# Feed-forward first product on scaled fp16 halves, with weight sums formed by adding transfers

## Chip, cores and metric

The kernel runs as one program on one core of a Trainium2 chip. The metric is the device time of one launch in microseconds (us). Three runs of the kernel before gave 2275.92 to 2276.97 us, median 2276.76.

## What is computed

Two layers of an encoder on 1024 positions of width 1024, fp32 in and out. Each layer is attention with a convolution module beside it, then a gated feed-forward block:

```
y = concatenate([y_attn, u]) @ w_o[l];  x = x + y
h2 = rmsnorm(x, g_ffn[l])
z = dwconv(h2 @ w_up[l], w_dw_ffn[l], b_dw_ffn[l])     # w_up: 1024 x 5632
zg, zv = split(z, 2)
x = x + (silu(zg) * zv) @ w_down[l]                    # w_down: 2816 x 1024
```

The change concerns `h2 @ w_up[l]`, the feed-forward block's first product.

## The kernel before

**Exact products from parts.** A fp32 operand is split into a high part, rounded to the reduced fp32 type F32R, and a low part, the rest. A product is three matmuls: high by high, high by low, low by high.

**Seven products for eight.** For block f (of 22: 128 gate columns and 128 value columns) the weights lie as four quarters, gate or value (e = 0, 1) by half of the contraction (h = 0, 1). A scheme of Strassen's kind makes two halves of the positions of both gate and value from seven products instead of eight, in the order `ORDER = (1, 5, 6, 3, 7, 2, 4)`. Products 1, 2 and 4 take a quarter as it is; 5, 6, 3 and 7 take sums and differences of quarters (weights) and of quarters of h2 (the "mixed sets" 5, 3, 6, 7, 4). Products 6, 7, 4 and 3 add onto a PSUM bank that already holds an earlier product of the block, so that the eviction in between (`evict`, L1124) must come first. One product is 12 matmuls of 128x128 by 128x512 (`product`, L1112 to L1122; the matmul is L1120) and fills one *step*.

**Order.** `feed` (L899) has a list of steps, TensorE's work, and a table of work put behind a step with a rank, written out by hand: `put(step, rank, f)`. Every engine's queue runs in program order. Steps 0 to 15 are the w_o stage (`wo_steps`, L933), where h2 is normed (`norm`, L996; `first`, L1001, for sets 1 and 2 in steps 12 to 15) and the mixed sets are made (`combine`, L1006, at the steps of `MIX_AT`, 18 to 31). Then 154 steps are the up-projection (`up_steps`, L1061): first those of `START` (L90: products 1 and 2 of blocks 0 to 3, then the others of blocks 0 to 3 as their sets come), then block after block. Below, n is the step of a block's product 1. The down-projection follows (`down_steps`, L1238), in the same scheme with its own combinations (`combine`, L1283) and evictions (`evict_end` L1316, `evict` L1327).

**Weights of blocks 4 to 21.** SP's queue fetches both rows of quarters (512 KB each, `fetch`, L1071) at n - 8. VectorE forms the sums in place (L1078, through `sub`, L1069). Products 5 and 6 take their parts from `pair` (L1494): ScalarE rounds, VectorE subtracts (L1499). Products 3 and 7 (`part`, L1082) and 1, 2 and 4 (`cast` and `turn`, L1093) get the low part by a transfer: a GpSimd DMA writes the high part, rounding on the way (`cast_pair`, L891, DMA at L894), or ScalarE does; then `complete` (L188) has ScalarE write the high part's negative (L189) and a GpSimd DMA add the source to it from HBM (L190).

**Beside it.** In eleven blocks of each layer (7 to 12 and 14 to 18) a pair of rows of the down weights is loaded (`sum_load`, L1170), summed in four steps on VectorE (`sum_step`, L1175) and stored for the later stage. The convolution over z, silu and the product of gate and value run on ScalarE and VectorE (L1146 to L1168). In the mixing stage, `value_squares` and `value_scale` (L858, L866) make a power-of-two scale for the attention's value weights from the sum of their squares; TensorE sums over partitions by a matmul with ones (L870).

Of the kernel before, what the change touches and what calls it, by code (L numbers as in the profile page):

```python
# [9 lines left out]
F32 = mybir.dt.float32  # L10
# [40 lines left out]
P_GKV = 11  # L51
# [20 lines left out]
P_SCALE = 32768.0  # L72
TURNED_BY_DMA = ()
# [23 lines left out]
TAIL_STEPS = 6  # L97
ENDS = (slice(512, 768), slice(768, T))
# [27 lines left out]
class Encoder:  # L126
# [257 lines left out]
    def run(self):  # L384
# [4 lines left out]
        self.ones = self.cp.tile([128, 128], F32, name="ones")  # L389
        nc.vector.memset(self.ones, 1.0)  # L390
        self.ones_r = self.cp.tile([128, 128], F32R, name="ones_r")
# [9 lines left out]
    def first_sections(self, l, supply):  # L401
# [58 lines left out]
        nc.vector.tensor_copy(out=self.ones_r, in_=self.ones)  # L460
# [87 lines left out]
    def project(self, l, carry):  # L548
# [264 lines left out]
        scales = {1: lambda: st.update(squares=self.value_squares(l, w["v"])),  # L813
                  2: lambda: st.update(scale=self.value_scale(l, st.pop("squares")))}
# [43 lines left out]
    def value_squares(self, l, w):  # L858
        f = self.cp.tile([128, 8], F32, name=f"vf{l}", tag="vf", bufs=1)
        for k in range(2):  # L860
            t = self.blk(f"vsq{l}_{k}")[:, 0:512]
            self.nc.scalar.activation(out=t, in_=w[0][:, k * 512:(k + 1) * 512].bitcast(F32), func=AF.Square,
                                      scale=self.par[l][:, P_GKV + k:P_GKV + k + 1], accum_out=f[:, k:k + 1])
        return f

    def value_scale(self, l, f):  # L866
        nc = self.nc
        ps = self.bank(f"vf{l}p", (128, 1))
        for k in range(2):
            nc.tensor.matmul(ps, self.ones, f[:, k:k + 1], start=k == 0, stop=k == 1)  # L870
        h, s, r = (f[:, i:i + 1] for i in (2, 3, 4))
        nc.vector.tensor_scalar(out=h.bitcast(I32), in0=ps.bitcast(I32), scalar1=24, scalar2=None, op0=ALU.logical_shift_right)
        nc.vector.tensor_scalar(out=s.bitcast(I32), in0=h.bitcast(I32), scalar1=-8388608.0, scalar2=200 * 8388608.0, op0=ALU.mult, op1=ALU.add)
        nc.vector.tensor_scalar(out=r.bitcast(I32), in0=h.bitcast(I32), scalar1=8388608.0, scalar2=39 * 8388608.0, op0=ALU.mult, op1=ALU.add)
        return s, r
# [57 lines left out]
    def wo_steps(self, l, conv, ys, w, casts, x, steps, put):  # L933
        nc, a, par = self.nc, self.a, self.par[l]
        left, right = HALVES
        casts, ps, acc, sq, rf, us = {(1, m): e for m, e in casts.items()}, {}, {}, {}, {}, []
# [59 lines left out]
        def norm(c, k):  # L996
            xk = x[k, c]
            nc.vector.scalar_tensor_tensor(out=xk, in0=xk, scalar=par[:, P_GFFN + k:P_GFFN + k + 1], in1=rf[c],
                                           op0=ALU.mult, op1=ALU.mult)

        def first(k):  # L1001
            norm(0, k)
            i = 1 + k // 4
            sets[i].append(self.pair(x[k, 0], f"b{l}_{i}{k}", "m", True))

        def combine(i, ks, srcs):  # L1006
            for o, p, q in srcs:
                if q is not None:
                    nc.vector.tensor_tensor(out=o, in0=p, in1=q, op=ALU.subtract)
            pairs = [self.tmp("b", f"b{l}_{i}{k}", F32R, (128, 2, 512)) for k in ks]  # L1010
# [31 lines left out]
        for k in range(8):  # L1042
# [6 lines left out]
        plan = ((5, 0, b11, b12, b11), (3, 4, b22, b22, None), (6, None, b11, b22, b11), (7, None, b12, b22, b12),  # L1049
                (4, None, b21, b21, b11))  # L1050

        def mix(i, j, o, p, q, ks):
            for k in ks if j is not None else ():
                norm(1, k + j)
            combine(i, ks, [(o(k), p(k), q(k) if q else None) for k in ks])
# [5 lines left out]
    def up_steps(self, l, steps, put):  # L1061
# [6 lines left out]
        raw, wts, casts, st, sums = defaultdict(dict), {}, {}, defaultdict(dict), {}  # L1068
# [6 lines left out]
        def quarters(f):  # L1075
            return [raw[f][e][:, h] for e in range(2) for h in HALVES]

        def combine(f, o, p, q, op=ALU.subtract):  # L1078
            z = quarters(f)
            sub(z[o], z[p], z[q], op)  # L1080

        def part(i, f):  # L1082
            a11, a12, a21, a22 = quarters(f)
            src = {1: a11, 2: a12, 5: a21, 6: a21, 7: a11, 3: a12}[i]
            if i == 7 or f < 2 or i == 3 and f >= LEFT:
                t = self.tmp("ws", f"w{l}_{f}_{i}", F32R, (128, 2, 512))
                nc.scalar.copy(out=t[:, 0], in_=src)
                self.complete(None, t[:, 0], t[:, 1], src)
            else:
                t = self.pair(src, f"w{l}_{f}_{i}", "ws")  # L1090
            wts[i, f] = t[:, 0], t[:, 1]

        def cast(i, f):  # L1093
            e, h = {1: (0, 0), 2: (0, 1), 4: (1, 1)}[i]
            casts[i, f] = self.cast_pair(a["w_up"][l, f + e * NF][:, HALVES[h]], f"w{l}_{f}_{i}", "b" if i == 4 and f >= LEFT else "ws")

        def turn(i, f):
            wts[i, f] = self.complete(*casts.pop((i, f)))

        def first_cast(f):  # L1100
            casts[f] = self.cast_tile(a["w_up"][l, f], f"wc{l}_{f}", "b" if f == 1 else "ws")

        def first_turn(f):
            hi, lo = self.complete(*casts.pop(f))
            for i, c in enumerate(HALVES):
                wts[1 + i, f] = hi[:, c], lo[:, c]
# [5 lines left out]
        def product(i, f):  # L1112
            z, w = st[f], wts.pop((i, f))
            if i in (1, 5, 2):
                z[i] = bank(i, f)
            ps = z[{6: 1, 7: 1, 4: 1, 3: 5}.get(i, i)]
            for k in range(4):
# [6 lines left out]
        def evict(i, f):  # L1124
            z = st[f]
            if i == 1:
                z["g"] = self.blk(f"zg{l}_{f}")
                nc.scalar.copy(out=z["g"][:, left], in_=z[1])
            elif i == 5:
                z["v"] = self.blk(f"zv{l}_{f}")  # L1130
                nc.scalar.copy(out=z["v"][:, right], in_=z[5])
            elif i in (6, 3):
                src = z[1] if i == 6 else z.pop(5)
                if (i == 3) == (f < LEFT):
                    nc.scalar.copy(out=z["g"][:, right], in_=src)
                else:
                    sub(z["g"][:, right], src, z["g"][:, right], ALU.add)
            elif i == 7:
                sub(z["v"][:, right], z[1], z["v"][:, right], ALU.add)
            elif i == 2:  # L1140
                sub(z["g"][:, left], z.pop(2), z["g"][:, left], ALU.add)
            elif i == 4:
                nc.scalar.copy(out=z["v"][:, left], in_=z.pop(1))

        def filter_start(f, e):
            z = st[f]  # L1146
# [4 lines left out]
        def filter_tap(f, e, t):  # L1151
            z = st[f]
            self.conv_tap(l, e * NF + f, z["ov"[e]], z["in", e], 0, T, t)

        def keep(f):
            st[f]["src"] = st[f].pop("v")

        def silu(f):
            o = st[f]["o"]
            nc.scalar.activation(out=o, in_=o, func=AF.Silu)  # L1160

        def close(f):
            z = st.pop(f)
# [19 lines left out]
        for f, e, n, tag in ((0, 0, 4, "wr"), (1, 0, 5, "wr"), (0, 1, 6, "wr"), (1, 1, 9, "b"),  # L1183
                             (2, 1, 22, "b"), (2, 0, 22, "b"), (3, 0, 24, "b"), (3, 1, 24, "wr")):
            put(n, 5, lambda f=f, e=e, tag=tag: fetch(f, e, tag))
        for f in range(1, LEFT):
            n = 10 + f if f == 1 else 11 + f
            put(n, 4, lambda f=f: first_cast(f))
            put(n + 2 + f // 3, 4, lambda f=f: first_turn(f))
        for i in (1, 2):  # L1190
            put(13, 0.5, lambda i=i: part(i, 0))
        for q, (i, f) in enumerate(seq):
# [4 lines left out]
            if i == 4 or i < 3 and f >= LEFT:  # L1197
                early = 2 if i == 4 and f < 2 else 0
                put(n - (9 if f >= LEFT else 7) - early, 1.5, lambda i=i, f=f: cast(i, f))
                put(n - 5 - early, 4, lambda i=i, f=f: turn(i, f))  # L1200
            elif i > 2 and f < LEFT:
                m = {5: 18, 3: 20, 6: 24, 7: 27}[i] if f < 2 else n - {5: 3, 3: 4, 6: 6, 7: 6}[i]
                put(m, 0.5 if f < 2 else 4, lambda i=i, f=f: part(i, f))
                if i == 5:
                    put(17 if f < 2 else m - 1, (0.5 if f < 2 else 3), lambda f=f: (combine(f, 0, 0, 2), combine(f, 2, 2, 3, ALU.add)))
# [736 lines left out]
```

## Time and profile before

| | |
|---|---|
| median of three runs | 2276.76 us |
| the profiled execution | 2276.63 us |
| its span, first to last instruction | 2274.9 us |
| granted TensorE clock, mean | 0.999 |
| w_o stage, layer 0 / 1 | 406 to 504 / 1533 to 1632 us |
| up-projection | 504 to 926 / 1632 to 2053 us |
| down-projection | 926 to 1137 / 2053 to 2267 us |

How to read the profile: PE is TensorE's matmuls, PEld its weight loads, DVE VectorE, ACT ScalarE, POOL GpSimd, SP the engine that only issues DMAs. "L1120" is the line of the kernel's file. A group's row reads line, engine, operation, output <- inputs, shape, count, then busy time, mean length of one in ns, and idle time ahead of it with what ended it. A matmul's own length overlaps the next one's: what counts is the distance from start to start. Of the DMA queues, q0 is GpSimd's software queue and q1 the hardware queue of SP; "to landing" is from issue to completion.

### The profile page before, as it was taken

Reading aid. Unit: us, or ns where it says so; the run is one execution under the profiler, and the core shown is the slowest. Engines: PE = TensorE matmul, PEld = TensorE weight load, DVE = VectorE, ACT = ScalarE, POOL = GpSimd, SP = SyncE. Lnnn points to the kernel's source line nnn. Section 1 sums busy time; section 2 is a strip of 40 time slices with the busy share of each in tenths; the row PEclk is TensorE's granted clock in tenths of the full one; section 3 lists DMA queues with packets and bytes.
Section 4 is the critical chain, followed back from the end, with each engine's and each line's share of the span. In section 5 each row is a group of like instructions: output and inputs, shape, how many; then the busy total and the mean of one; then the engine's idle time right before and its main releaser. Section 6 shows DMA issues by size and latency. Waiting matters only on the chain.

```text
span 2274.9 us, 30440 instructions
## 1 busy us (share of the span) xinstructions
PE 2264.2 (100%) x10690; PEld 1834.8 (81%) x10690; DVE 1738.7 (76%) x2305; ACT 1298.0 (57%) x2058; POOL 783.0 (34%) x812
## 2 busy tenths in 40 slices
PE   9999999999999999999999999999999999999999
PEld 8887777788888888888888877777888888888888
DVE  7989888868877676776559788887697777768765
ACT  5355977646655555544533578784475555555444
POOL 1222797532333333001412237963323333320032
PEclk9999999999999999999999999999999999999999
DMA  6888998856899998935968999867669999989356
GB/s 194 168 180 260 199 207 177 212 151 141 208 281 297 275 297 203 333 106 144 207 139 167 215 255 201 188 150 208 174 132 231 269 300 278 294 208 320 105 121 171
DMA packets 199144, 475.72 MB, mean 209 GB/s; under 512 B 27232, under 2 KB 35280, under 8 KB 198992
## 3 DMA queue, kind: packets, MB, share of 16 engines
q0 software_dynamic: 103136, 222.46, 48.6%
q1 hardware_dynamic: 95568, 250.80, 32.9%
q8 instruction: 84, 1.38, 0.3%
q14 instruction: 68, 0.56, 0.1%
q10 hardware_dynamic: 288, 0.53, 0.1%
HBM read 309.29 MB, written 80.40 MB: 171 GB/s over the span
## 4 chain that ended last, share of the span: by engine, by line
PE 93%; issue 2%; DVE 2%; DMA 1%; ACT 1%; SPq 0%; POOL 0%; DVEq 0%; POOLq 0%; ACTq 0%
PE p L1120 36%; PE pd L1308 18%; PE po L931 7%; PE s L1564 7%; PE t L1604 4%; PE o L1627 4%; PE pq L226 3%; PE pa L226 3%; PE pkv L226 2%; PE pg L226 2%; PE pg L545 2%; PE pa L545 1%; PE pk L226 1%; PE pn L226 1%; PE pkr L759 1%
## 5 line engine op out<-in xcount | busy, mean ns | idle before, releaser
L1120 PE MATMUL p<-b,w 128*128 128x512 f32 x3552 | 807.0, 389 | 0.6 <-DVE zv L1069 0.5
L1120 PEld LDWEIGHTS p<-b,w 128*128 128x128 f32 x3552 | 666.3, 188 | 140.6 <-DVE zv L1069 0.9
L1308 PE MATMUL pd<-ab,wd 128*128 128x512 f32 (+1 forms) x1920 | 422.2, 381 | 0.0
L1308 PEld LDWEIGHTS pd<-ab,wd 128*128 128x128 f32 x1920 | 350.8, 188 | 69.4 <-DVE ab L1499 0.4
L190 POOL DMA_DIRECT2D w<-wu x96 | 84.8, 886 | 360.5 <-ACT w L189 310.0
L1564 PE MATMUL s<-k,q 96*128 96x512 f32 x768 | 207.7, 406 | 0.8 <-ACT p L1574 0.8
L1607 DVE SCALAR_TENSOR_TENSOR pt<-t,pt 128x512 f16<-128x512 f32 x256 | 164.8, 684 | 38.9 <-ACT pt L1606 38.3
L1796 POOL TENSOR_TENSOR late<-gate,par 128x1014 f32<-128x1014 f32 (+12 forms) x79 | 171.6, 2172 | 12.4 <-PE pn L226 12.4
L1606 ACT ACTIVATE pt<-t 128x512 f16<-128x512 f32 x256 | 139.2, 596 | 57.0 <-PE t L1604 56.0
L1511 DVE SCALAR_TENSOR_TENSOR o<-zg,par,o 128x1023 f32<-128x1023 f32 x88 | 112.8, 1283 | 76.5 <-ACT o L1505 75.2
L190 POOL DMA_DIRECT2D w<-in_w_up x116 | 100.5, 867 | 199.2 <-ACT w L189 175.3
L1566 DVE TENSOR_REDUCE mx<-s 128x1 f32<-128x1024 f32 x128 | 155.7, 1217 | 1.3 <-PE s L1564 1.3
L1564 PEld LDWEIGHTS s<-k,q 96*128 96x128 f32 x768 | 135.2, 189 | 23.6 <-ACT p L1574 1.3
L1574 ACT ACTIVATE p<-s,mx 128x1024 f32<-128x1024 f32 x128 | 143.2, 1118 | 4.4 <-DVE mx L1566 4.0
L1779 DVE SCALAR_TENSOR_TENSOR conv<-gate,par,conv 128x1009 f32<-128x1009 f32 (+7 forms) x112 | 142.3, 1274 | 3.7 <-ACT conv L607 1.0
L1604 PEld LDWEIGHTS t<-ident,p 128*128 128x128 f32 x1024 | 119.8, 141 | 25.2 <-DVE yt L1634 0.8
L894 POOL DMA_DIRECT2D wd<-in_w_down x44 | 32.8, 754 | 306.6 <-PE pd L1308 306.4
L1497 ACT CAST ab<-ac 128x512 fp32r<-128x512 f32 x130 | 80.1, 617 | 97.5 <-DVE ac L1243 94.8
L189 ACT ACTIVATE w<-w 128x512 fp32r<-128x512 f32 x212 | 133.5, 630 | 3.0
L1627 PE MATMUL o<-pt,v 128*128 128x512 f16 x512 | 132.8, 381 | 1.2 <-DVE pt L1607 1.1
L1604 PE MATMUL t<-ident,p 128*128 128x128 f32 x1024 | 133.2, 273 | 0.1
L1069 DVE TENSOR_TENSOR zg<-p,zg 128x512 f32<-128x512 f32 x88 | 60.5, 690 | 95.1 <-PE p L1120 88.4
(2117 smaller groups left out, 4083.9 us busy)
## 6 DMA issues: line engine op xcount, KB each, us to landing
w<-in_w_up POOLq DMA_DIRECT2D x232, 256.0 KB, 7.3
wu<-in_w_up SPq DMA_DIRECT2D x88, 512.0 KB, 5.7
w<-wu POOLq DMA_DIRECT2D x96, 256.0 KB, 5.9
sd<-in_w_down SPq DMA_DIRECT2D x44, 512.0 KB, 9.9
ws<-sd SPq DMA_DIRECT2D x44, 512.0 KB, 7.0
wd<-in_w_down POOLq DMA_DIRECT2D x88, 256.0 KB, 5.4
act<-v SPq DMA_DIRECT2D x36, 512.0 KB, 5.8
ac<-act SPq DMA_DIRECT2D x72, 256.0 KB, 6.1
```

The source lines that it names most:

```text
L190: self.nc.gpsimd.dma_start(out=lo, in_=src, accum_op=ALU.add)
L226: nc.tensor.matmul(ps[:, HALVES[c]], w, x[:, HALVES[c]], start=(k == 0 and s == 0), stop=(k == n - 1 and s == 2))
L931: self.nc.tensor.matmul(ps, p[:, sl], q[:, cs], start=(k == 0 and t == 0), stop=(k == 3 and t == 2))
L1120: nc.tensor.matmul(ps, w[p][:, k * 128:(k + 1) * 128], b[:, q], start=(i in (1, 5, 2) and k == 0 and t == 0), stop=(k == 3 and t == 2), sk ...
L1308: nc.tensor.matmul(ps[t, m][:, cs], w[i, j][p][:, m * 128:(m + 1) * 128], b[:, q, cs], start=(i in (1, 5, 2) and j == 0 and s == 0), stop= ...
L1564: nc.tensor.matmul(ps[:, cs], q[i][0:96, qs], k[j][0:96, cs], start=(s == 0), stop=(s == 2))
L1566: nc.vector.tensor_reduce(out=mx, in_=ps, op=ALU.max, axis=AX.X, negate=True)
L1574: nc.scalar.activation(out=p, in_=ps, func=AF.Exp, bias=mx, accum_out=st["sums"][:, qt:qt + 1])
L1604: nc.tensor.transpose(tp[:, i, qi * 128:(qi + 1) * 128], st["p"][2 * qp + qi][:, kt * 128:(kt + 1) * 128], self.ident)
L1607: nc.vector.scalar_tensor_tensor(out=lo, in0=tp, scalar=P_SCALE, in1=hi, op0=ALU.mult, op1=ALU.subtract)
L1627: nc.tensor.matmul(po, v[2 * c + i][:, h // 2, e, :], pt[s][:, 2 * (c % 2) + i, :], start=(c == 0 and i == 0 and s == 0), stop=(c == 3 and ...
L1796: self.nc.gpsimd.tensor_tensor(out=p[:, lo:hi], in0=u[:, lo + s:hi + s], in1=self.tap(l, j, t).broadcast_to([128, hi - lo]), op=ALU.mult)
```

## The change

1. **fp16 parts.** The products of L1120 take fp16 high and low parts of both operands. h2 is scaled by a power of two through its gain (`scales`, from the squares of the gain, in the same small matmul as the value weights' scale). Each block's weights get a power-of-two scale from the sum of their squares: two Squares of 1,024 columns on ScalarE, a matmul with ones, five one-column operations on VectorE. ScalarE writes the scaled high part (`upper`), VectorE the low part (`lower`). The evictions multiply the scale back out. No part of w_up is cast or completed by transfer any more.
2. **Value rows' sign turned.** Some products, and the quarters of z that they make, carry the other sign, so that every sum of weight quarters is an addition. The down-projection's combinations and evictions turn it back.
3. **Sums by adding transfers.** The sums for products 5, 6, 3 and 7 are formed by GpSimd DMAs that add a quarter from HBM to the fetched one in SBUF. The down weights' sums are formed by GpSimd DMAs that add one half in SBUF to another, four per pair of rows; step offsets 0, 3, 3, 6 and 9 (the store) in place of 1, 1, 2 and 6.
4. **Mixed sets.** The low parts of all sets are subtracted on GpSimd (before: sets 1 and 2 alone).
5. **Blocks 0 to 3.** Their rows are fetched at steps 0 to 4, squared two steps later, and have one sum and one set of scales at step 7; they are fetched a second time for the sums.
6. **Times.** For blocks 4 to 21: fetch n - 14, squares n - 11 and n - 10, first sum n - 10, total n - 8, scale n - 7, parts from n - 7 to n + 3.

The core of the diff:

```diff
         def combine(i, ks, srcs, sign):
...
-                if i in MIX_ADDED:
-                    self.complete(None, t[:, 0], t[:, 1], src[0])
-                else:
-                    nc.vector.tensor_tensor(out=t[:, 1], in0=src[0], in1=t[:, 0].bitcast(F32), op=ALU.subtract)
+                nc.gpsimd.tensor_tensor(out=t[:, 1], in0=src[0], in1=t[:, 0], op=ALU.subtract)
...
+        def add_in(dst, src):
+            nc.gpsimd.dma_start(out=dst, in_=src, accum_op=ALU.add)
+
+        def sum5(f):
+            add_in(raw[f][1][:, left], block(f, 1, 1))
...
+        def squares(f, e, out):
+            t = self.blk(f"wsq{l}_{f}{e}", F16)
+            nc.scalar.activation(out=t, in_=raw[f][e], func=AF.Square, accum_out=out)
...
+        def own_total(f):
+            st["total", f] = self.pp.tile([128, 2], F32, name=f"wt{l}_{f}", tag=f"d{6 + (f > LEFT and (f + 1) % 2)}", bufs=1)
+            nc.tensor.matmul(st["total", f], self.ones, st["sums", f][:, 6:8], start=True, stop=True)
...
+        def upper(t, src, f):
+            nc.scalar.activation(out=t, in_=src, func=AF.Copy, scale=scale[f])
+
+        def lower(t, src, hi, f):
+            nc.vector.scalar_tensor_tensor(out=t, in0=src, scalar=scale[f], in1=hi, op0=ALU.mult, op1=ALU.subtract)
...
         def sum_step(j, n):
             p, q = sums[j]
-            sub(*((p[:, left], p[:, left], p[:, right]), (p[:, right], p[:, right], q[:, right], ALU.add),
-                  (q[:, right], q[:, right], p[:, left]), (q[:, left], q[:, left], q[:, right]))[n])
-            if n == 3:
-                for e, t in enumerate(sums.pop(j)):
-                    nc.sync.dma_start(out=self.wsd[l][j, e], in_=t)
+            if n < 4:
+                add_in(*((p[:, left], p[:, right]), (p[:, right], q[:, right]), (q[:, right], p[:, left]), (q[:, left], q[:, right]))[n])
+                return
+            for e, t in enumerate(sums.pop(j)):
+                nc.sync.dma_start(out=self.wsd[l][j, e], in_=t)
...
         for f in range(LEFT, NF):
-            n = at[1, f]
+            n = at[1, f] + 2 * (f == LEFT)
             for e in range(2):
...
+                at_step(n - 14, 5 + e / 10, fetch, f, e, "b" if e else "wr")
+                at_step(n - 11 + e, 2, own_squares, f, e)
+            at_step(n - 10, 2.1, sum5, f)
+            at_step(n - 8 + (f == LEFT), 0.4, own_total, f)
+            at_step(n - 7 + (f == LEFT), 0.5, own_scale, f)
+            for i, m in ((5, -6 if f == LEFT else -7), (6, -3), (4, -2), (3, 1), (7, 2)):
+                at_step(n + m, 3.6, part_hi, i, f)
+                at_step(n + m + 1, 3.5 if i != 6 else 1, part_lo, i, f)
+                if i in (5, 6):
+                    at_step(n + m + 1, 3.55, (sum6, sum3)[i - 5], f)
```

More of the change, by code (lines that the diff above doesn't have):

```diff
@@ L866, in value_scale @@
-    def value_scale(self, l, f):
-        nc = self.nc
[L868 to L875, printed above, removed]
+            nc.scalar.activation(out=t, in_=w[0][:, k * 512:(k + 1) * 512].bitcast(F32), func=AF.Square,
+                                 scale=par[:, P_GKV + k:P_GKV + k + 1], accum_out=f[:, k:k + 1])
@@ L1067, in up_steps @@
         self.kept = {}
-        raw, wts, casts, st, sums = defaultdict(dict), {}, {}, defaultdict(dict), {}
+        raw, wts, zs, st, sums, scale, back, nback = defaultdict(dict), {}, defaultdict(dict), {}, {}, {}, {}, {}
         sub = lambda o, p, q, op=ALU.subtract: nc.vector.tensor_tensor(out=o, in0=p, in1=q, op=op)
@@ L1093, in cast, with block @@
[L1093 to L1106, printed above, removed]
+        def block(f, e, h):
+            return a["w_up"][l, f + e * NF][:, HALVES[h]]
@@ new lines, in scales @@
+        def scales(ps, out, w):
+            ps = ps.rearrange("p (f e) -> p f e", e=2)
+            scale, back, nback, v, h = (out[:, i * w:(i + 1) * w] for i in range(5))
+            nc.vector.tensor_reduce(out=v, in_=ps, op=ALU.add, axis=AX.X)
+            self.half_exponent(h, v)
+            self.power(scale, h, -1.0, 204.0)
+            for o, at in ((back, self.back), (nback, self.nback)):
+                nc.vector.tensor_scalar(out=o.bitcast(I32), in0=h.bitcast(I32), scalar1=EXPONENT, scalar2=at, op0=ALU.mult, op1=ALU.add)
+            return scale, back, nback
@@ new lines, in first_total, with first_squares @@
+        def first_total():
+            ps = self.bank(f"wt{l}", (128, 2 * LEFT))
+            tags = self.banks[1][0]
+            tags.insert(0, tags.pop())
+            nc.tensor.matmul(ps, self.ones, st["sums"], start=True, stop=True)
+            parts = scales(ps, self.cp.tile([128, 5 * LEFT], F32, name=f"wt{l}", tag="wt", bufs=1), LEFT)
+            for f in range(LEFT):
+                scale[f], back[f], nback[f] = (t[:, f:f + 1] for t in parts)
+        def first_squares(f, e):
+            if "sums" not in st:
+                st["sums"] = self.cp.tile([128, 2 * LEFT], F32, name=f"wa{l}", tag="wa", bufs=1)
+            squares(f, e, st["sums"][:, 2 * f + e:2 * f + e + 1])
@@ new lines, in upper, with part_hi, part_lo, both @@
+        def upper(t, src, f):
+            nc.scalar.activation(out=t, in_=src, func=AF.Copy, scale=scale[f])
+        def lower(t, src, hi, f):
+            nc.vector.scalar_tensor_tensor(out=t, in0=src, scalar=scale[f], in1=hi, op0=ALU.mult, op1=ALU.subtract)
+        def part_hi(i, f):
+            upper(operand(i, f)[:, 0], source(i, f), f)
+        def part_lo(i, f):
+            hi, lo = wts[i, f]
+            lower(lo, source(i, f), hi, f)
+        def both(f):
+            return st[(1, 2), f], raw[f][0].rearrange("p (i c) -> p i c", i=2)
@@ L1108, in bank, with first_hi, first_lo @@
+        def first_hi(f):
+            for i in (1, 2):
+                operand(i, f)
+            t, src = both(f)
+            upper(t[:, :, 0], src, f)
+        def first_lo(f):
+            t, src = both(f)
+            lower(t[:, :, 1], src, t[:, :, 0], f)
         def bank(i, f):
```

211 lines of the change are left out of this document (126 added, 85 removed).

## The prediction

> **What bounds the kernel now.** First the engine totals and the chain of waits of the profile before.
>
> ```profile
> PE 2264.2 (100%) x10690; PEld 1834.8 (81%) x10690; DVE 1738.7 (76%) x2305; ACT 1298.0 (57%) x2058; POOL 783.0 (34%) x812
> ...
> PE 93%; issue 2%; DVE 2%; DMA 1%; ACT 1%; SPq 0%; POOL 0%; DVEq 0%; POOLq 0%; ACTq 0%
> PE p L1120 36%; PE pd L1308 18%; PE po L931 7%; PE s L1564 7%; PE t L1604 4%; PE o L1627 4%; PE pq L226 3%; PE pa L226 3%; PE pkv L226 2%; PE pg L226 2%; PE pg L545 2%; PE pa L545 1%; PE pk L226 1%; PE pn L226 1%; PE pkr L759 1%
> ```
>
> TensorE is busy all through, and its own instructions are 93% of the chain that ends last; the line that the change rewrites, L1120, is 36% of the span. Every nanosecond of TensorE's cadence counts, and other work costs something only where it makes TensorE wait. The table by stage shows, for layer 0, the four stretches that the change reaches: the w_o stage, the start of the up-projection, its steady part, and the down-projection.
>
> ```profile
> 406.00:504.00 98.00, 97.29 (x452) 78.83 (x451) 67.30 (x104) 46.36 (x74) 38.73 (x42) 1.00 0.67 184
> 504.00:583.00 79.00, 78.92 (x353) 64.86 (x352) 69.42 (x105) 52.23 (x86) 21.39 (x28) 1.00 0.69 156
> 583.00:926.00 343.00, 342.48 (x1511) 283.25 (x1510) 244.42 (x300) 191.85 (x290) 103.99 (x137) 1.00 0.97 266
> 926.00:1137.00 211.00, 211.00 (x936) 174.74 (x936) 146.04 (x231) 102.26 (x178) 35.43 (x50) 1.00 0.66 189
> ```
>
> Columns: stretch, its length, busy time of TensorE, of its weight load, of VectorE, ScalarE and GpSimd, the granted clock (1.00, so no throttle), the DMA engines' busy share, GB/s. In the start, VectorE is at 69.42 of 79 us. In the steady part it is at 244.42 of 343 and ScalarE at 191.85, but the DMA engines are at 0.97: the resource that is closest to taking over from TensorE.
>
> **TensorE's own part.** The timeline of TensorE has one row with 45 products of L1120 in a run, and one with eight fp16 matmuls of the same size in a run, each with weights of its own; the groups give the length of one:
>
> ```profile
> 695.83 10.36 PE L1120 MATMUL p<-b,w 128*128 128x512 f32 x45
> ```
>
> ```profile
> 412.50 1.89 PE L1627 MATMUL o<-pt,v 128*128 128x512 f16 x8
> ```
>
> ```profile
> L1120 PE MATMUL p<-b,w 128*128 128x512 f32 x3552 | 807.0, 389 | 0.6 <-DVE zv L1069 0.5
> ...
> L1627 PE MATMUL o<-pt,v 128*128 128x512 f16 x512 | 132.8, 381 | 1.2 <-DVE pt L1607 1.1
> ```
>
> From start to start a fp32 matmul takes (10.36 - 0.389) / 44 = 226.6 ns, a fp16 one (1.89 - 0.381) / 7 = 215.6 ns. The program has 22 blocks x 7 products x 12 matmuls x 2 layers = 3,696 of them, and as many after. Gain: 3,696 x 11.0 ns = **-40.7 us**.
>
> Added on TensorE are the sums of squares over partitions: a matmul of ones with two or eight columns, 18 + 1 per layer, 38 in all; the two calls per layer that sum the value weights' squares become one, so 36 more calls. The nearest rows are those two present calls, four passes, in TensorE's timeline:
>
> ```profile
> 191.18 0.50 PE L870 MATMUL vf0p<-vf,ones 128*128 128x1 f32 x4
> 191.54 0.72 PE L226 MATMUL pn<-cqs_0h,wu10h 128*128 128x512 f32 x2
> ```
>
> The next product starts 0.36 us after the first pass, so 0.18 us per call: 36 x 0.18 = **+6.5 us**. The sums go beside nothing; all of it counts.
>
> **VectorE, ScalarE, GpSimd.** The groups, each form apart, give the price of one operation:
>
> ```profile
> L1607 DVE SCALAR_TENSOR_TENSOR pt<-t,pt 128x512 f16<-128x512 f32 x256 | 164.8, 684 | 38.9 <-ACT pt L1606 38.3
> ...
> L1574 ACT ACTIVATE p<-s,mx 128x1024 f32<-128x1024 f32 x128 | 143.2, 1118 | 4.4 <-DVE mx L1566 4.0
> ...
> L189 ACT ACTIVATE w<-w 128x512 fp32r<-128x512 f32 x212 | 133.5, 630 | 3.0
> ...
> L1499 DVE TENSOR_TENSOR ab<-ac,ab 128x512 fp32r<-128x512 f32 x130 | 89.2, 688 | 22.7 <-ACT ab L1497 15.6
> ...
> L1574 ACT ACTIVATION_READ_ACCUMULATOR p<-s,mx 128x1 f32 x128 | 26.8, 209 | 0.0
> ...
> L1499 POOL TENSOR_TENSOR b<-y,b 128x512 fp32r<-128x512 f32 x16 | 24.2, 1625 | 28.1 <-ACT b L1497 28.1
> ...
> L745 DVE SCALAR_TENSOR_TENSOR qn<-qn,qns 128x1024 fp32r<-128x1024 f32 x8 | 15.5, 1944 | 2.4 <-ACT qns L743 2.4
> ...
> L1779 DVE SCALAR_TENSOR_TENSOR conv<-gate,par,conv 128x1020 f32<-128x1020 f32 x8 | 10.2, 1279 | 0.2
> ```
>
> VectorE loses 264 sums of weight halves, 84 lows of weights and 40 of mixed sets (0.69 us each), and gains 220 lows of 512 columns (0.684, as L1607, fp16 out as well), 44 of 1,024 (1.28, as L1779) and some 190 one-column operations (taken at 0.21, the shortest row here): -268 + 150 + 56 + 40 = -22 us. ScalarE loses 212 negations and some 186 casts (0.63), and gains 220 scaled uppers of 512 columns (0.63), 44 of 1,024 and 88 squares of 1,024 (1.12, and 0.21 to read the accumulator): -251 + 139 + 49 + 117 = +54 us. Both are spread over some 840 us of products. In the steady part neither comes near TensorE's pace: nothing, unless one of these in-order queues stands at a transfer, since the eviction that TensorE needs before it adds to a bank again is queued behind it (see the chain of transfers).
>
> GpSimd takes over 20 lows of mixed sets per layer, in the start. L745 runs while GpSimd combines tensors and has a mean of 1.94 us, where L1779, as wide and also with both inputs in SBUF, takes 1.28 us: the two engines hinder each other. The Trainium skill, "SBUF — State Buffer", section "Who interferes with whom", has the rule: a VectorE instruction with two SBUF inputs contends with a GpSimd instruction that reads SBUF, and the one that comes second waits out the whole instruction. The two means agree; no row shows it in the start, and the rule speaks against this move. The price in both layers: at best nothing (20 x 0.69 = 13.8 us per layer leave VectorE). At worst VectorE waits out each, 20 x 1.625 = 32.5 us, against 79 - 69.4 + 13.8 = 23.4 us of room: 9 us per layer, **18 us** in all. I take **+3 us**, near the lower end: sets are mixed at steps 18 to 31 of the stage, three to six steps (12 x 0.2266 = 2.72 us each) ahead of their products, so most of the waiting fits. In this are the eight squares per layer in the w_o stage, where ScalarE has 98 - 46 = 52 us of room.
>
> Turned signs in the down-projection change operators, not counts (0.69 us before and after): nothing.
>
> **DMA.** Two windows of the transfers: four blocks of the steady part, in each of which a half of the down weights is summed as well, and a cast that stands alone (4 us).
>
> ```profile
> DMA packets 8418, 22.33 MB, mean 290 GB/s; under 512 B 932, under 2 KB 932, under 8 KB 8412
> ...
> q0 software_dynamic: 4605, 8.39, 53.0%
> q1 hardware_dynamic: 3807, 13.87, 50.1%
> ...
> w<-in_w_up POOLq DMA_DIRECT2D x24, 256.0 KB, 9.5
> wu<-in_w_up SPq DMA_DIRECT2D x8, 512.0 KB, 7.2
> ws<-sd SPq DMA_DIRECT2D x8, 512.0 KB, 8.3
> sd<-in_w_down SPq DMA_DIRECT2D x8, 512.0 KB, 10.5
> w<-wu POOLq DMA_DIRECT2D x10, 256.0 KB, 7.3
> act<-v SPq DMA_DIRECT2D x4, 512.0 KB, 6.5
> ```
>
> ```profile
> q0 software_dynamic: 144, 0.26, 24.5%
> ...
> wd<-in_w_down POOLq DMA_DIRECT2D x1, 256.0 KB, 3.0
> ```
>
> The window (773 to 850 us) is 77 us long. A hardware transfer of 512 KB takes 0.501 x 77 / 28 = 1.38 us of all engines; 34 software transfers take 0.530 x 77 / 34 = 1.20 us each. A cast alone took 0.245 x 4 = 0.98 us; with 12 casts among the 34, an adding transfer takes (40.8 - 11.8) / 22 = 1.32 us. Per such block before: 5 adding, 3 casts, 7 hardware = 6.6 + 2.9 + 9.7 = 19.2 us against TensorE's 84 x 0.2266 = 19.0. After: 4 adding for the up-weights, 4 for the down-weights' sums, the same 7: 10.6 + 9.7 = **20.2 us against 84 x 0.2156 + 0.18 = 18.3**. (The shares add to 103% in that window, because packets of both queues overlap on an engine, so 1.03 is what was carried without loss.) At 1.03 a block takes 19.6 us, 1.3 more than TensorE: there are 11 of them per layer, in runs of six and five, and the seven others need only 4 adding and 3 hardware transfers (9.4 us) and make up ground. Bounds: nothing, if more than 1.03 can be carried or the lag stays in the lead (fetches are issued 14 steps ahead, each sum three steps, 7.8 us, ahead of its reader), up to 2 x (11 x 1.3 - 2 x 1.3) = **23 us**, with only 7.8 - 6.5 = 1.3 us of lead per run (6.5: next row). No row says where between, so I take the middle: **+11 us**.
>
> **The chain of transfers on GpSimd.** The adding transfers' line in the steady part:
>
> ```profile
> L190 POOL DMA_DIRECT2D w<-wu x34: 889/893/1255, 601.2 to 906.6; - x34
> ...
>   ACT w L189: 200.4, 81
> ...
> DMA to landing us min/median/max: 3.3/6.5/10.0
> ```
>
> GpSimd spends 200 us there waiting for ScalarE's negations; these waits go. New ones come: the down weights' sums are formed in place by transfers, each needing the one before: the second must have landed before the third writes what the second reads, and so on. All issue from GpSimd's one in-order queue, so a block takes at least 3 landings plus an issue of 0.9 us; queued behind are the up-weights' sums, which ScalarE waits for, then evictions, then TensorE. At 18.3 us the break-even is a landing of (18.3 - 0.9) / 3 = **5.8 us**. The median of before, 6.5, lies above; but it was reached with several transfers under way, (24 x 9.5 + 10 x 7.3) / 77 = 3.9 by the window's rows, and in the chain each starts with one or two ahead of it. Nearer to it is the middle between 3.3 and 6.5, 4.9 us: 15.6 us a block, hidden. Cost: nothing, upper bound in rival C.
>
> **Sum.** Against the profiled execution, 2276.63 us (its span is 2274.9; the median of the runs is 0.13 higher): 2276.6 - 40.7 + 6.5 + 3 + 11 = **2256 us**.
>
> **Rivals.**
> The page's DMA issues, both layers:
>
> ```profile
> w<-in_w_up POOLq DMA_DIRECT2D x232, 256.0 KB, 7.3
> ...
> w<-wu POOLq DMA_DIRECT2D x96, 256.0 KB, 5.9
> ```
>
> H, all hidden: 2276.6 - 40.7 + 6.5 = 2242 us. For it: VectorE gets lighter and the transfers of the whole stage fewer (88 + 44 adding per layer in place of (232 + 96) / 2 = 164 software transfers). Against: 20.2 us of transfers in 18.3.
> S, the start stalls: VectorE and GpSimd lock each other out at their worst, 2242 + 11 + 18 = 2271 us. For it: 69.42 of 79 and L745's mean. Against: the room of some steps.
> C, slower than before: the chain on GpSimd takes the place of TensorE as the bound. With a landing of 6.5 us a block takes 20.4 us, 2.1 over; 2 x (11 x 2.1 - 2 x 1.3) = 41 us: 2242 + 3 + 41 = 2286 us, and with 7.3 us (w<-wu in the window above) 4.5 us a block, 94 us, 2339. It decides from 5.8 us on.
> N, the change doesn't do what it says: fp16 holds 215.6 ns only over eights, and in long runs keeps 226.6. 2276.6 + 6.5 + 11 = 2294 us at most. Against: no row shows what would hold it back.
>
> **How the numbers follow.** Chances: forecast 0.34 (own range 2248 to 2267), H 0.17, S 0.12, C 0.29, N 0.05, worse than all 0.03. About 0.2%, 4.5 us, can be told from no change: from 2272.2 to 2281.3. Faster: forecast, H and 0.07 of S, 0.58. Same: 0.05 of S and 0.04 of C (landing just over the break-even), 0.09. Slower: 0.25 of C, N and the rest, 0.33. The range runs from H to a C at 6.6 us: 2241 to 2292; beyond lie 0.10 of C, half of N and the rest, and a little of H, 0.18.
>
> **What would show it.** Products at about 215.6 ns in long runs and 38 small sums near 0.18 us (else N). In the dense windows of the steady part, idle TensorE with ScalarE waiting for the transfers into the raw weights: by full DMA engines (share 0.99, GpSimd not waiting) the forecast; with GpSimd standing at the down weights' landings, C. Idle TensorE in the start before (3, 0), (6, 0) with lows late on GpSimd: S. The forecast is wrong if TensorE is idle under 3 us in all or over 30.

## The result and the profile after

The changed kernel takes 2372.73 us (median of four runs, 2370.92 to 2374.02) against 2276.86 us for the kernel before: ratio 1.042, 95% interval 1.0402 to 1.0438. It is 96 us slower, where 21 us less was forecast; the range ended at 2292.

The page of the changed kernel: engine totals, the chain that ended last, and the groups and transfers that answer to those shown of before (L1208 is the product, L1099 all adding transfers, L1169 and L1172 the high and low parts of the weights).

```profile
PE 2270.6 (96%) x10762; PEld 1517.9 (64%) x10762; DVE 1759.2 (74%) x2384; ACT 1364.9 (58%) x2104; POOL 803.8 (34%) x776
...
PE 62%; DMA 16%; issue 8%; DVE 6%; POOL 5%; ACT 4%; POOLq 0%; SPq 0%; DVEq 0%; ACTq 0%
PE pd L1405 18%; DMA sd<-sd 11%; PE p L1208 11%; PE s L1665 6%; PE po L949 4%; PE t L1705 4%; PE o L1728 3%; DMA wu<-in_w_up 3%; PE pq L228 3%; PE pa L228 3%; PE pkv L228 2%; PE pg L228 2%; DVE w L1172 2%; PE pg L546 1%; POOL sd L1099 1%
...
L1208 PE MATMUL p<-b,w 128*128 128x512 f16 x3696 | 843.6, 389 | 83.3 <-ACT zg L1215 60.3
...
L1099 POOL DMA_DIRECT2D sd<-sd x88 | 78.2, 953 | 268.9 <-DMA sd<-sd 259.2
...
wu<-in_w_up POOLq DMA_DIRECT2D x176, 256.0 KB, 7.0
...
sd<-sd POOLq DMA_DIRECT2D x88, 256.0 KB, 7.9
```

TensorE's share of the chain falls from 93% to 62%, and the line that bounded the kernel from 36% to 11%. In its place stands a transfer, `sd<-sd`, the down weights' sums: 11%, and GpSimd waits 259 us for them. The table by stage, for layer 0 again:

```profile
406.00:510.00 104.00, 102.84 (x479) 81.48 (x477) 76.31 (x115) 57.71 (x93) 41.04 (x45) 1.00 0.71 199
510.00:590.00 80.00, 70.24 (x314) 31.14 (x313) 58.62 (x77) 46.68 (x72) 34.16 (x31) 0.96 0.41 92
590.00:970.00 380.00, 347.11 (x1568) 155.87 (x1567) 258.16 (x351) 220.22 (x305) 100.79 (x114) 0.96 0.88 224
970.00:1182.00 212.00, 212.00 (x941) 175.13 (x939) 145.88 (x231) 102.98 (x179) 34.97 (x50) 1.00 0.66 184
```

The loss lies in the up-projection: TensorE idles 10 us in the start and 33 us in the steady part, and the granted clock, 1.00 before, is 0.96 in both. VectorE and ScalarE are far from full. Six blocks of the steady part (7 to 12), one row each:

```profile
656.90:675.10 18.20, 18.20 (x87) 8.39 (x88) 13.53 (x19) 12.34 (x17) 5.25 (x6) 1.00 0.89 205
675.10:693.40 18.30, 18.30 (x90) 8.49 (x89) 13.71 (x19) 12.12 (x17) 5.72 (x8) 1.00 0.95 246
693.40:718.90 25.50, 20.74 (x90) 8.97 (x89) 13.62 (x19) 12.34 (x17) 8.45 (x10) 0.87 0.99 255
718.90:738.60 19.70, 18.65 (x87) 8.31 (x88) 13.71 (x19) 12.34 (x17) 6.61 (x8) 1.00 0.97 254
738.60:761.10 22.50, 18.67 (x89) 8.31 (x88) 13.81 (x19) 12.32 (x17) 6.43 (x9) 1.00 0.97 252
761.10:784.60 23.50, 19.82 (x89) 8.75 (x88) 13.71 (x19) 12.36 (x18) 7.68 (x10) 0.93 0.99 255
```

Blocks without a hold-up take the forecast 18.3 us. Sums start at block 7; after two blocks the lead is used up and a block takes 19.7 to 25.5 us. GpSimd's timeline over a block shows what paces it (each row a group of issues, in brackets the wait ahead of it):

```profile
720.33 1.78 POOL L1099 DMA_DIRECT2D sd<-sd  x2 [2.80 <-DMA sd<-sd]
725.07 0.88 POOL L1099 DMA_DIRECT2D wu<-in_w_up  x1 [2.96 <-DVE w L1172]
731.72 0.89 POOL L1099 DMA_DIRECT2D sd<-sd  x1 [5.77 <-DMA sd<-sd]
735.53 0.88 POOL L1099 DMA_DIRECT2D sd<-sd  x1 [2.93 <-DMA sd<-sd]
736.07 3.06 POOL L1099 DMA_DIRECT2D wu<-in_w_up  x3
743.40 1.78 POOL L1099 DMA_DIRECT2D sd<-sd  x2 [4.27 <-DMA sd<-sd]
```

In the order of the queue the first row is the fourth sum of one pair and the first of the next; 731.72 is the second, 735.53 the third, 743.40 the fourth. Each of these three is issued when the one before has landed: from row to row 11.4, 3.8 and 7.9 us, 23.1 in all, against 18.3 us of TensorE's work in a block. The three up-weight sums at 736.07 had to stand behind the third. This is rival C.

### The profile page after: what moved, and what is told of

Read it like the earlier page. It is cut to its first block, busy times and chain, and to the rows that moved or that the text cites. A ratio compares the mean times of both kernels' runs of the same rounds, so it can differ in the third digit from the quotient of the medians.

```text
span 2372.2 us, 30272 instructions
## 1 busy us (share of the span) xinstructions
PE 2270.6 (96%) x10762; PEld 1517.9 (64%) x10762; DVE 1759.2 (74%) x2384; ACT 1364.9 (58%) x2104; POOL 803.8 (34%) x776
## 4 chain that ended last, share of the span: by engine, by line
PE 62%; DMA 16%; issue 8%; DVE 6%; POOL 5%; ACT 4%; POOLq 0%; SPq 0%; DVEq 0%; ACTq 0%
PE pd L1405 18%; DMA sd<-sd 11%; PE p L1208 11%; PE s L1665 6%; PE po L949 4%; PE t L1705 4%; PE o L1728 3%; DMA wu<-in_w_up 3%; PE pq L228 3%; PE pa L228 3%; PE pkv L228 2%; PE pg L228 2%; DVE w L1172 2%; PE pg L546 1%; POOL sd L1099 1%
## 5 line engine op out<-in xcount | busy, mean ns | idle before, releaser
L1208 PE MATMUL p<-b,w 128*128 128x512 f16 x3696 | 843.6, 389 | 83.3 <-ACT zg L1215 60.3
L1208 PEld LDWEIGHTS <-w 128*128 128x128 f16 x3696 | 367.6, 101 | 544.3 <-issue 112.6
L1099 POOL DMA_DIRECT2D wu<-in_w_up x176 | 160.6, 1060 | 373.0 <-DVE w L1172 273.8
L1169 ACT ACTIVATE w<-wu,wf 128x512 f16<-128x512 f32 (+1 forms) x216 | 162.9, 785 | 165.7 <-DMA wu<-in_w_up 155.6
L1172 DVE SCALAR_TENSOR_TENSOR w<-wu,wf,w 128x512 f16<-128x512 f32 (+1 forms) x216 | 177.6, 834 | 87.2 <-ACT w L1169 87.0
L1099 POOL DMA_DIRECT2D sd<-sd x88 | 78.2, 953 | 268.9 <-DMA sd<-sd 259.2
L1612 DVE SCALAR_TENSOR_TENSOR v<-zv,par,v 128x1023 f32<-128x1023 f32 x88 | 112.4, 1280 | 32.5 <-ACT v L1606 32.5
```

Of the source, the lines that this page charges most:

```text
L1099: nc.gpsimd.dma_start(out=dst, in_=src, accum_op=ALU.add)
L1169: nc.scalar.activation(out=t, in_=src, func=AF.Copy, scale=scale[f])
L1172: nc.vector.scalar_tensor_tensor(out=t, in0=src, scalar=scale[f], in1=hi, op0=ALU.mult, op1=ALU.subtract)
L1208: nc.tensor.matmul(ps, w[p][:, k * 128:(k + 1) * 128], b[:, q], start=(i in (1, 5, 2) and k == 0 and t == 0), stop=(k == 3 and t == 2), sk ...
```

## Experiments

Each kernel ran beside the kernel before (2276.1 to 2276.8 us there); the ratios are to it.

**1. The two suspects.** e1 forms the sums on VectorE, e2 spreads the transfers, e3 puts the mixed sets' lows back on VectorE, e4 is e1 and e3. All start from the changed kernel.

```diff
 e1
-                add_in(*((p[:, left], p[:, right]), ...)[n])
+                o, i = ((p[:, left], p[:, right]), ...)[n]
+                sub(o, o, i, ALU.add)
...
-            for i, d in enumerate((0, 3, 3, 6, 9)):
+            for i, d in enumerate((1, 1, 2, 6, 6)):
 e2
-            for i, d in enumerate((0, 3, 3, 6, 9)):
+            for i, d in enumerate((0, 4, 8, 12, 16)):
 e3
-                nc.gpsimd.tensor_tensor(out=t[:, 1], in0=src[0], in1=t[:, 0], op=ALU.subtract)
+                nc.vector.tensor_tensor(out=t[:, 1], in0=src[0], in1=t[:, 0], op=ALU.subtract)
```

> The changed kernel (2372.7 us), with the down weights' four sums formed by VectorE additions again instead of adding transfers (step offsets 1, 1, 2, 6 and the store at 6, as before the change). In the changed kernel's trace blocks 9 to 13 and 15 to 19 take 18.8 to 25.6 us where the others take 18.3: 41 us of excess in layer 0 and 44 in layer 1. Theory A (the serial chain of adding transfers in GpSimd's queue holds up the up-weights' sums) and theory B (the DMA engines are simply full) both expect the excess gone, about 2290 us, with every such block at 18.3 us. Theory C (fp16 parts, scales and their queues on ScalarE and VectorE cost the time) expects less than 20 us off, above 2350.

2289.46 us, ratio 1.0055 (1.004 to 1.007): 83 us less. Theory A or B of this expectation, not its theory C (fp16; not the rival C of the prediction).

> The changed kernel with the same adding transfers for the down weights' sums, but at step offsets 0, 4, 8, 12 and the store at 16 instead of 0, 3, 3, 6, 9, so that each has landed (10.5 us of cover against a landing of 7.6) when GpSimd's queue comes to its follower. Bytes and transfers are the same. Theory A (waits in GpSimd's queue) expects most of the 85 us of excess gone: 2290 to 2310 us, GpSimd's wait for sd at a tenth of its 259 us. Theory B (full DMA engines, 20 us of transfers in a block of 18.3) expects blocks at 19.6 us or more still, 2320 us or above; if B holds alone, no change, 2372.

2294.9 us, ratio 1.0086 (1.0069 to 1.0103): 78 us less with the same transfers. Theory A; full engines (B) leave at most the 5.4 us to e1. The new offsets also changed the order of SP's queue; part 4 comes back to this. The longest waits of GpSimd in the whole of e2 are these, and a wait for `sd` on another sum is nowhere left among its waits:

```profile
POOL wu L1099 <- DVE w L1172: 324.3, 86, 23.2
POOL wd L912 <- PE pd L1405: 321.3, 13, 145.0
```

Blocks 10 to 12 of e2 fit in 18.3 to 19.3 us with DMA shares of 1.03 to 1.08. The prediction took 1.03 for the most that was known to be carried; that was the mean from 773 to 850 us, and within it one block of the kernel before (823 to 842 us) already had a share of 1.08 with TensorE busy throughout. The three blocks of e2:

```profile
715.00:733.30 18.30, 18.30 (x90) 8.49 (x89) 13.60 (x19) 11.69 (x17) 5.82 (x9) 1.00 1.08 305
733.30:752.20 18.90, 18.51 (x90) 8.39 (x89) 13.35 (x20) 11.66 (x18) 6.72 (x9) 1.00 1.08 300
752.20:771.50 19.30, 18.48 (x87) 8.35 (x88) 13.71 (x20) 12.23 (x17) 6.86 (x9) 1.00 1.03 265
```

> The changed kernel with the low parts of the mixed sets subtracted on VectorE again, GpSimd's share only sets 1 and 2 as before the change. The steps of the start, blocks 0 to 4, are 22 us over 2.6 each per layer. The theory that VectorE and GpSimd lock each other out there expects most of it gone, 25 to 40 us less: 2333 to 2348. The rival (the start waits for late transfers and for the order of ScalarE's queue, whichever engine subtracts) expects a change under 8 us, and VectorE's 20 more operations of 0.69 us per layer could even cost some.

2355.46 us, ratio 1.0345 (1.033 to 1.036): 17 us less, between the two expectations. The lows of the weights beside them, L1172 on blocks 0 to 3, show the hold-up: in the changed kernel, then in e3, by form,

```profile
L1172 DVE SCALAR_TENSOR_TENSOR w<-wu,wt,w 128x512 f16<-128x512 f32 x40 | 46.1, 1171 | 34.0 <-ACT w L1169 34.0
```

```profile
L1172 DVE SCALAR_TENSOR_TENSOR w<-wu,wt,w 128x512 f16<-128x512 f32 x40 | 31.1, 794 | 11.0 <-ACT w L1169 11.0
```

the same 40 operations with two inputs in SBUF take 1171 ns beside GpSimd's subtractions and 794 with most of these gone.

> Both at once: down weights' sums and the lows of the mixed sets on VectorE again, everything else as in the changed kernel. If the two costs are apart, their gains add: about 2372.7 - 82 - 32 = 2259 us, between the floor of 2242 and the kernel before at 2276.8. If VectorE then becomes too full in the start or in the blocks with sums, it stays above 2277.

2273.78 us (ten runs), ratio 0.9986 (0.9977 to 0.9996). The gains add (83 + 17 = 100 expected, 99 measured), but 31 us remain over the floor of 2242.

**2. One part alone, one landing fewer, and the rest of the start.** e5 is e4 with two shifts; e6 puts the transfers into the kernel before; e7 forms only the first sum on VectorE; e8 is e2 and e3.

```diff
 e5
-                for i, m in ((5, (15, 24)[h]), ...
+                for i, m in ((5, (16, 24)[h]), ...
...
-            for i, m in ((5, -6 if f == LEFT else -7), ...
+            for i, m in ((5, -6 if f <= LEFT + 1 else -7), ...
 e7
-                add_in(*((p[:, left], p[:, right]), ...)[n])
+                o, i = ((p[:, left], p[:, right]), ...)[n]
+                if n == 0:
+                    sub(o, o, i, ALU.add)
+                else:
+                    add_in(o, i)
```

> The version with both on VectorE (2273.8 us) with two shifts by one step: the parts of product 5 of blocks 0 and 1 at step 16 in place of 15, and the high part of product 5 of block 5 at n - 6 in place of n - 7. In its trace 13 us per layer are still lost at six places of the start. Two of them are read as in-order queues: product (2, 0) stands 2.9 us behind the norm's statistics, which VectorE forms after two lows that GpSimd holds up; products 6 and 3 of block 4 stand 5.7 us behind evictions that ScalarE does after it has waited 3.8 us for block 5's scale. If so, up to 2 x 8.6 = 17 us go: 2257 to 2266. If the waits only move to the next place: 2270 or above.

2261.07 us, ratio 0.9927 (0.9911 to 0.9944): 13 of the 17 us. The two shifts were not run apart. It is the fastest of all kernels here, 0.7% under the kernel before.

> The kernel before the change (2276.6 us), fp32 products and all, with one part of the change alone: the down weights' sums by adding transfers at step offsets 0, 3, 3, 6 and 9. The sums' signs are left wrong (the transfers can only add). If the serial chain in GpSimd's queue is a cost of its own, three landings of 7 us or more and an issue are 22 us or more against a block of 19.05: 11 x 3 us per layer less some lead, 2320 to 2360 us. The rival, that it hurts only together with fp16 and the new up-weight sums (here the casts and completions have four steps of cover each), expects 2267 to 2287.

2404.79 us, ratio 1.0562 (1.0547 to 1.0578): 128 us slower, more than expected. Two of its waits over the whole kernel, and its steady part in layer 0:

```profile
POOL sd L1179 <- DMA sd<-sd: 263.7, 52, 9.1
```

```profile
DVE wu L1069 <- DMA wu<-in_w_up: 158.9, 25, 9.6
```

```profile
583.00:926.00 343.00, 305.57 (x1270) 246.31 (x1269) 185.15 (x218) 162.90 (x245) 128.14 (x162) 0.94 1.00 259
```

GpSimd waits as long for `sd` as in the changed kernel, so the transfers cost without fp16 and without the new up-weight sums. How much of the 128 us is the chain stays open, because this run does not set it apart from full DMA engines. By the prices of the prediction a block with sums now has 9 adding transfers, 3 casts and 7 hardware transfers, 11.9 + 2.9 + 9.7 = 24.5 us of all engines against TensorE's 19.0. Over 22 such blocks that is an estimate of some 120 us, and the DMA share is 1.00 over the whole stretch. The 159 us of VectorE waiting are for SP's fetches; what held these up was not tried.

> The changed kernel with only the first of the four down-weight sums on VectorE, the other three adding transfers as they were, offsets unchanged. The serial chain is then two landings and an issue, 2 x 7.6 + 0.9 = 16.1 us, under a block's 18.3: theory A expects nearly all of the 83 us gone that the version with all four on VectorE gained, 2290 to 2310. If the cost goes by the number of transfers, three quarters remain: about 2352.

2327.9 us, ratio 1.0223 (1.0208 to 1.0238): 45 us less, between both expectations. Its GpSimd over a block:

```profile
718.62 0.88 POOL L1099 DMA_DIRECT2D sd<-sd  x1 [4.59 <-DMA wu<-in_w_up]
722.38 0.88 POOL L1099 DMA_DIRECT2D wu<-in_w_up  x1 [2.88 <-DVE w L1172]
722.92 1.24 POOL L1099 DMA_DIRECT2D sd<-sd  x1
729.87 0.88 POOL L1099 DMA_DIRECT2D sd<-sd  x1 [5.71 <-DMA sd<-sd]
...
738.45 0.89 POOL L1099 DMA_DIRECT2D sd<-sd  x1 [3.83 <-DMA sd<-sd]
```

Two landings take 6.9 and 8.6 us, and ahead of the second sum (722.92) stands an up-weight sum that waits for VectorE's low part, 3.8 us after 718.62. Together 19.8 us, over 18.3: fewer landings, but in this block other waits of the same queue come into the ring.

> Transfers spread (offsets 0, 4, 8, 12, 16) and the lows of the mixed sets on VectorE, in one kernel: if the two costs are apart, 2294.9 - 17.3 = 2278 us, 2 to 6 us over the version with sums and lows on VectorE (2273.8), which is then the price of carrying the sums by transfer in full DMA engines. If the spread transfers bind once the start is faster: 2285 or above.

2275.11 us (ten runs), ratio 0.9992 (0.9982 to 1.0001): 1.3 us over e4. The costs of the chain and of the lows are apart.

**3. What else paces the queue.** e9 spaces the transfers by three steps, e10 is e5 with spread transfers, e11 is e7 with one swap.

```diff
 e9
+            for i, d in enumerate((0, 3, 6, 9, 12)):
 e10
+            for i, d in enumerate((0, 4, 8, 12, 16)):
 e11
+            for i, d in enumerate((0, 3, 4, 6, 9)):
```

> The changed kernel with its adding transfers at offsets 0, 3, 6, 9 and the store at 12: only the third no longer follows the second at once, all are three steps (7.9 us) apart, against landings of 7.6 in the changed kernel and 8.9 where they were four steps apart. If it is the waiting in GpSimd's queue that costs, this lies near the run with four steps (2294.9), a little above it since some landings exceed 7.9 us: 2295 to 2320. If the amount of transfers per block were the cause, it stays at 2372.

2346.13 us, ratio 1.0307 (1.0291 to 1.0322): only 27 us less; the expectation missed. Three steps, 7.9 us, are the median landing, and landings reach far over it: the line L1099 of the changed kernel, steady part, has

```profile
DMA to landing us min/median/max: 3.3/7.8/13.9
```

so the wait comes back in many blocks: from 600 to 960 us GpSimd still waits 77 us for `sd`. With four steps, 10.5 us, that wait is gone (e2). In e9 ScalarE's squares also wait 26 us for SP's fetches, and the sums 23 us for SP's loads of the down weights; the changed kernel has no such waits in that stretch, so a part of the 51 us between e9 and e2 may be SP's.

> The best version so far (sums and lows on VectorE, two shifts, 2261.1 us) with the sums by adding transfers four steps apart in place of VectorE. Without the shifts the two ways gave 2275.1 and 2273.8, so 2262 +- 4 here, if the price of the transfers stays about 1 us; if the start's faster pace runs into full DMA engines, 2268 or above.

2264.71 us, ratio 0.9944 (0.9928 to 0.9961): 3.6 us over e5. That is the price of carrying the sums by transfer when GpSimd's queue does not wait for them.

> The kernel with one sum on VectorE (2327.9 us) and one swap in GpSimd's queue: the first up-weight sum of the block after next is issued ahead of the third down-weight sum, not behind it (offset 4 in place of 3). There, blocks still took 20.3 us although two landings make 16.1; read from its queue, a second loop binds: up-weight sum, down-weight sum's landing, next block's first up-weight sum, its landing of 10 us, high and low part, next up-weight sum. With the swap the first landing drops out of that loop: 2290 to 2305 expected. If the loop is not the cause, 2320 or above.

2326.76 us, ratio 1.0223 (1.0207 to 1.0238): no change. The theory of that one loop falls. Its queue:

```profile
703.53 1.24 POOL L1099 DMA_DIRECT2D wu<-in_w_up  x1
704.07 1.61 POOL L1099 DMA_DIRECT2D sd<-sd  x1
711.22 0.88 POOL L1099 DMA_DIRECT2D wu<-in_w_up  x1 [5.54 <-ACT wsq L1115]
711.76 1.24 POOL L1099 DMA_DIRECT2D sd<-sd  x1
...
723.20 0.88 POOL L1099 DMA_DIRECT2D sd<-sd  x1 [7.40 <-DMA sd<-sd]
```

The wait for VectorE is gone as expected (703.53 follows at once), but the third sum now stands behind one more transfer and its follower comes after 11.4 us in place of 8.6: in this block, what the swap gave, the longer landing took.

**4. SP's store.** SP waits for the last landing before it stores the sums, with later loads behind it; e12 (from the changed kernel), e13 (e9) and e14 (e7) put the store at a later step, e15 (e2) at an earlier one.

```diff
 e12 and e14
+            for i, d in enumerate((0, 3, 3, 6, 13)):
 e13
+            for i, d in enumerate((0, 3, 6, 9, 16)):
 e15
+            for i, d in enumerate((0, 4, 8, 12, 13)):
```

> The changed kernel (2372.7 us) with one thing moved: the store of the down weights' sums at offset 13 in place of 9, the four adding transfers at 0, 3, 3, 6 as they were. In SP's queue this store waits for the last sum's landing (219.9 us of waiting in the steady part of layer 0), and the loads of the next weights stand behind it, come in a burst, and land after 10 to 12 us. If that is the loop that holds the blocks at 20 to 25 us: 50 us or more less, 2300 to 2325. If GpSimd's own chain of three landings is enough: 2360 to 2380.

> The transfers three steps apart (0, 3, 6, 9; 2346.1 us with the store at 12) with the store at 16. If SP's store is the loop, it comes near the run with four steps and the store at 16 (2294.9): 2295 to 2310. If the spacing on GpSimd decides, it stays at 2340 to 2350.

> The kernel with the first sum on VectorE (2327.9 us) with the store at 13 in place of 9. SP loop: 2290 to 2305. GpSimd's two landings, or the loop through the up-weights' sums: unchanged, 2322 to 2333.

> The transfers four steps apart (0, 4, 8, 12), the store at 13 in place of 16, one step after the last transfer is issued. If SP's store is the loop, the gain of the spread goes again: 2330 or above, against 2294.9. If the spacing on GpSimd decides: 2290 to 2300.

2371.98, 2346.35, 2326.87 and 2295.37 us; ratios 1.0415 (1.0399 to 1.043), 1.0306 (1.0291 to 1.0323), 1.0222 (1.0205 to 1.0239) and 1.0084 (1.0069 to 1.0099). Each is within 1.1 us of its base, but this decides nothing about SP, because the edits did not reach its queue. The table of steps and ranks sets the order of the four engines in the kernel's list `MANUAL` (L80 of the changed kernel: TensorE, VectorE, ScalarE, GpSimd). SP is not in it, so the order by the table, told ahead of the prediction of every engine's queue, does not hold for SP. In the traces of e12 to e15 every engine issues the same instructions in the same order as in its base. SP's wait in the steady part stays too, first in the changed kernel, then in e12:

```profile
SPq L1268 <- DMA sd<-sd: 219.9, 33, 15.6
```

```profile
SPq L1268 <- DMA sd<-sd: 218.5, 33, 14.2
```

So the four runs are repeats, and show how closely a time comes back. What SP's wait costs has to be read from other rows. e1 and e7 leave the order of SP's queue as in the changed kernel, so their gains do not come from that order. From 600 to 960 us of the changed kernel, only three waits of a computing engine, 15 us in all, end with a transfer of SP's; GpSimd waits 121 us for the sums and ScalarE 75 us for GpSimd's up-weight sums. That speaks for GpSimd's queue. But no run tests it alone: e2 and e9 changed the order of SP's queue together with the spacing, and SP's loads come in bursts that may lengthen the landings of the sums.

## Why the prediction was wrong

- **The mechanism was named, as rival C; the step that failed is its price**: "Nearer to it is the middle between 3.3 and 6.5, 4.9 us: 15.6 us a block, hidden." The form, three landings and an issue per block, was right, but the landings were not at 4.9 us. In the steady part of layer 0 of the changed kernel the sums' transfers have

```profile
DMA to landing us min/median/max: 3.3/7.6/10.6
```

The median lies over the prediction's own break-even of 5.8 us; even the median of before, 6.5, did. In the block above the three landings are 10.6, 3.5 and 7.6 us. That each starts "with one or two ahead of it" holds for the second alone: the first is issued with four transfers of GpSimd's queue still under way, the third with none, but with the three up-weight sums that it held back right behind it. e1 and e2 put the term at 78 to 83 us where the sum had 0; C itself had 41 with a landing of 6.5 us and 94 with 7.3. C's formula says too much: with 7.6 us it gives 114 us.
- **Full DMA engines**, +11: they carried 1.08 where I took 1.03 for what was known (the kernel before had shown 1.08 in one block), and cost 5.4 us (e2 to e1), 1.3 (e8 to e4) and 3.6 (e10 to e5). Over-sized.
- **Lows on GpSimd**, +3: 17.3 us (e3) or 15.7 (e1 to e4), near the upper end of 18; "most of the waiting fits" was wrong. The Trainium skill's rule in "SBUF — State Buffer", section "Who interferes with whom", had spoken for that end; the 1171 and 794 ns above agree with it. VectorE's lows were under-priced as a whole: 1171 ns there and 745 in the other blocks in place of 684, and VectorE's total rose from 1738.7 to 1759.2 us where 22 us less was forecast.
- **Waits in in-order queues of the start**, taken at nothing: e5 moved two entries by a step and recovered 13 us; 19 us stay between e5 and the floor of 2242. Some 14 us of them are idle time of TensorE in the w_o stages, the starts and the steady parts; they were not taken apart further. For the start the prediction had priced only VectorE and GpSimd hindering each other, not the order of the queues.
- **fp16 cadence**, -40.7: right. One row of TensorE's timeline after:

```profile
518.66 18.08 PE L1208 MATMUL p<-b,w 128*128 128x512 f16 x83
```

(18.08 - 0.379) / 82 = 215.9 ns; 215.6 were forecast, and blocks that nothing holds up take 18.3 us with their small sum. In e5, 16 us of the gain come through.
- The sum of the terms: 2242 + 82 (chain) + 17 (lows) + 13 (shifts) + 19 (the rest) = 2373. The rest is what is left over, so the sum closes by construction.

## What to carry to other kernels

A transfer that needs another's landing is not work but a wait, and in an in-order queue everything behind it waits too: draw the ring of waits per block, price each landing by the queue that will stand ahead of it and by its longest cases, not by a quiet one, and space dependent transfers by more than that. The same transfers cost 83 us more than VectorE's additions, or only 1 to 5 us more, by the steps at which they were issued. Before a moved entry is taken for a test, see in the trace that the order really changed: here four edits left every queue as it was. When one engine is the bound for long, the gain of making it faster is only as large as the slack of every in-order queue that feeds it.

## What the hardware showed beyond this

A stall of TensorE can cost more than its length. Around the stall of block 12 in the changed kernel, the timeline and the windows say:

```profile
770.16 5.01 PE L1208 MATMUL p<-b,w 128*128 128x512 f16 x16 [3.68 <-ACT zg L1215]
```

```profile
770.20:772.90 2.70, 2.70 (x7) 0.95 (x7) 1.75 (x3) 2.33 (x3) 0.88 (x1) 0.50 1.08 301
772.90:778.00 5.10, 5.10 (x24) 2.25 (x23) 3.26 (x5) 4.04 (x6) 0.75 (x1) 0.99 1.11 251
```

After 3.7 us of idle time the granted clock is 0.50 for 2.7 us, in which 7 matmuls start, and then 0.99 again. Two more windows follow a stall of 2.33 us, which ends at 605.99, and one of 3.19 us, which ends at 747.14:

```profile
606.00:612.50 6.50, 5.51 (x13) 1.75 (x13) 3.79 (x5) 6.50 (x10) 0.87 (x1) 0.50 0.41 107
747.30:751.00 3.70, 3.70 (x18) 1.56 (x17) 2.75 (x4) 2.27 (x4) 0.88 (x1) 1.00 1.07 302
```

The Trainium skill, "TensorE: Matmul & The Clock Gate", section "What's actually happening", has a gate that halves the clock after an idle window of about 3.4 us and opens after a busy one; the trace agrees with the half. It shows no fixed length of stall: 3.68 and 2.33 us brought the half clock, 3.19 us did not. In the block of 25.5 us above, TensorE's busy time is 20.74 us at clock 0.87 against 18.3 undisturbed, so by this estimate 2.4 us of its 7.2 us of loss are the clock.
